# A transformer block on one NeuronCore: the attention's filling loaded and cast a tile in front, SyncE's queue in program order, and output pieces cast a product later

## The chip, the cores and the metric

One NeuronCore of a Trainium2 chip runs the whole program. The metric is the device time of one execution in microseconds; the median of several runs counts. The engines are TensorE (PE, matrix products), VectorE (DVE), ScalarE (ACT), GpSimd (POOL) and SyncE (SP, which here only issues transfers). Each works through its own instructions in their order, and they wait for one another by semaphores.

## The reference

One layer on x of 1 x 1024 x 1024 in float32:

```python
def reference(x, ...):
    h = rms_norm(x, ln1_g)
    proj = h @ w_in + b_in
    rq, rk, rv, rg, aq, ak, av, gate_a, gate_b = split(proj)  # 512 512 1024 1024 1024 128 128 1024 1024
    ry = head_group_norm(retention_chunkwise(rotary(rq), rotary(rk), rv), ret_norm_g)   # 4 heads
    branch_a = (silu(rg) * ry) @ w_ret_out
    ay = sliding_window_sink_attention(rotary(aq), rotary(ak), av, attn_sinks)  # 16 q, 2 kv heads, window 128
    branch_b = ay @ w_attn_out
    merged = sigmoid(gate_a) * branch_a + sigmoid(gate_b) * branch_b
    x = x + merged @ w_out
    h2 = rms_norm(x, ln2_g)
    x = x + (silu(h2 @ w_gate) * (h2 @ w_up)) @ w_down
    return rms_norm(x, lnf_g)
```

## The kernel before

Every float32 operand of a product is held as two numbers of a shorter format, a high part (a cast on ScalarE, the copy in `split`, line 133) and a low part (the difference, on VectorE, line 136). A product is the sum of three matmuls: high by high, high by low, low by high (lines 160 to 162 in `mm_g`). A weight slab of 1024 x 128 is loaded by SyncE into one of two raw buffers (`wr`), split into `wh` and `wl`, and used in 16 steps of three matmuls, eight steps for each half of the 1024 tokens.

The stage that the change concerns is the attention. The 16 query heads come in four quads. `quad_q(g)` makes the query projection of quad g: 32 steps on two slabs, with a rotation on VectorE (lines 440 to 449: six multiplies and adds and two low parts) for each half of the tokens. The results go out to `q_d` by four stores (line 452) and come back in another layout by four loads (line 453). `gate(n)` is one tile of the gates (16 steps), with a tanh whose result goes to `tb_d`.

Attention itself runs in 32 units (four quads by eight blocks of 128 queries). In turn i of the loop TensorE does `u_transpose` of unit i-2 (pT; ScalarE casts ph, VectorE makes pl at line 515 and the masked qh and ql at line 522), `u_scores` of unit i (s; exponentials at line 496), some steps of filling, and `u_values` of unit i-2 (pv, line 534, four matmuls that read ph, pl, qh and ql). From unit 16 on, `u_values` also adds halves and splits the sum on VectorE (lines 544 to 548). The filling is the projections of quads 1 to 3 and of twelve gate tiles, the gates 6 to 15, then 0 and 1: `Fill.step(n)` advances the generators by n steps, and `until(k)` runs them to the end of the k-th, so that a quad's queries are there when its first unit comes. TensorE's instructions are held in program order in this loop by `in_order`; SyncE's are placed by the scheduler. In turn 20 the four loads of `wv` (the retention's value weights) are issued, and in odd turns from 25 on VectorE subtracts quarters of it (line 593). What is left of the filling runs after the last unit (`fl.rest()`).

After the attention come the V products (va, vb; Strassen's scheme with seven products P1 to P7, whose sums of h VectorE makes into `vacc`, lines 660 and 663), then the W products of the retention's query, key and gate weights (wA, wB, wC; ten column blocks of seven products, 12 matmuls each, line 884). Their loop holds VectorE, ScalarE and GpSimd in program order. At the end of it, from product P6 of block 8 on, each product carries one piece of work for the attention's output: `split_ay(n)` reads a 128 x 512 piece of ay, adds its two parts on VectorE (`ays`, line 927), casts the sum on ScalarE (line 928), and one product later makes its low part on VectorE (line 922). Then follow `load_g(0)` and `k_transpose(0)` (kTT, transposes of the first retention head's keys) and the retention with the products of `w_attn_out` (acc_bb) as filling.

Of the kernel before, what the change touches and what calls it, by code (L numbers as in the profile page):

```python
# [17 lines left out]
P = 128  # L18
# [17 lines left out]
def f32(t):  # L36
    return t.bitcast(F32)
# [3 lines left out]
def hybrid_block(ctx: ExitStack, tc: tile.TileContext, x, ln1_g, w_in, b_in, ret_norm_g, w_ret_out,  # L41
# [262 lines left out]
    with tc.tile_pool(name="gt", bufs=1, side="right") as gt, tc.tile_pool(name="w1", bufs=1) as w1:  # L304
# [99 lines left out]
                ak_evac(q // 2, kb[q // 2])  # L404
                av_evac(q // 2, vb[q // 2])

        def quad_q(g):
            if g % 2 == 0:
                big(B, "B", g // 2, f"q{g}")
            Bt = B[g // 2]  # L410
            jb = (g % 2) * 4
            w = [hl_tiles([8, P], f"aq{g}{z}") for z in range(2)]
            hp = tc.high_priority(offset=AHEAD)
            hp.__enter__()
            for kk in range(2):
                raw = raw_slab([4, 256], f"aq{g}{kk}")
                nc.sync.dma_start(raw, w_in[kk * 512:kk * 512 + 512, C_AQ + g * 256:C_AQ + g * 256 + 256]
                                  .rearrange("(k p) n -> p k n", p=P))
                rv_ = raw.rearrange("p k (j z e) -> p k z j e", j=4, z=2, e=32)
                for z in range(2):  # L420
                    hi = w[z][0][:, kk * 4:kk * 4 + 4, :].rearrange("p k (j e) -> p k j e", e=32)
                    lo = w[z][1][:, kk * 4:kk * 4 + 4, :].rearrange("p k (j e) -> p k j e", e=32)
                    nc.scalar.copy(hi, rv_[:, :, z])
                    nc.vector.tensor_tensor(out=lo, in0=rv_[:, :, z], in1=f32(hi), op=ALU.subtract)
            hp.__exit__(None, None, None)
            ab = {}
            for half, z in ((0, 0), (0, 1), (1, 0), (1, 1)):
                pt = acc(f"aq{g}{z}{half}")
                yield from mm_g(pt, w[z], H, half * 512)
                t = r512("rab", 3, f"q{g}{z}{half}")  # L430
                nc.scalar.activation(t, pt, AF.Identity, bias=bcol[:, QB + 4 * z + g:QB + 4 * z + g + 1], scale=1.0)
                ab[z, half] = t
                if z == 0:
                    yield
                    continue
                c = slice(half * 512, half * 512 + 512)
                a, b = ab[0, half], t
                s1, s2 = (r512(f"st{i}", 1, f"st{i}{g}{half}") for i in (1, 2))
                cos, sin = atab[:, 0, c], atab[:, 1, c]
                nc.vector.tensor_tensor(out=s2, in0=a, in1=cos, op=ALU.mult)  # L440
                nc.vector.tensor_tensor(out=s1, in0=b, in1=sin, op=ALU.mult)
                nc.vector.tensor_tensor(out=s2, in0=s2, in1=s1, op=ALU.subtract)
                nc.vector.tensor_tensor(out=a, in0=a, in1=sin, op=ALU.mult)
                nc.vector.tensor_tensor(out=b, in0=b, in1=cos, op=ALU.mult)
                nc.vector.tensor_tensor(out=b, in0=b, in1=a, op=ALU.add)
                nc.scalar.activation(a.bitcast(F32R), s2, AF.Copy)
                nc.vector.tensor_tensor(out=s2.bitcast(F32R), in0=s2, in1=a, op=ALU.subtract)
                nc.scalar.activation(s1.bitcast(F32R), b, AF.Copy)
                nc.vector.tensor_tensor(out=b.bitcast(F32R), in0=b, in1=s1, op=ALU.subtract)
                qd = q_d[2 * g + half]  # L450
                for r, sr in ((0, a), (2, s2), (1, s1), (3, b)):
                    nc.sync.dma_start(qd[:, r, :], sr)
                    nc.sync.dma_start(f32(Bt[r * 32:r * 32 + 32, jb:jb + 4, c]),
                                      qd[:, r, :].rearrange("(j e) c -> e j c", e=32))
                yield
# [91 lines left out]
            nc.scalar.copy(v[:, :, 0, :], tm)  # L547
            nc.vector.tensor_tensor(out=v[:, :, 1, :], in0=tm, in1=f32(v[:, :, 0, :]), op=ALU.subtract)

        def gate(n):  # L550

            def evac(half, pt):
                t = gt.tile([P, 512], F32, tag="st", bufs=2, name=f"tb{n}{half}")
                nc.scalar.activation(t, pt, AF.Tanh, bias=bhalf[:, n:n + 1], scale=0.5)
                nc.sync.dma_start(tb_d[n, :, half * 512:half * 512 + 512], t)
            return dense_g(w_in, C_GA + n * P, H, evac, f"g{n}")

        run(quad_q(0))
        order = list(range(6, 16))
        gens = []  # L560
        for g in range(4):
            gens += [quad_q(g + 1)] if g < 3 else []
            gens += [gate(n) for n in (order[2 * g:2 * g + 2] if g < 3 else order[6:] + [0, 1])]
        fl = Fill(gens)
        NU = 4 * NB
        fl.step(20)
        left = 32 * 8 - 8 - 20
        with in_order(nc.tensor.engine):
            for i in range(NU + 2):
                if i % NB == 0 and 0 < i < NU:  # L570
                    fl.until(3 * (i // NB - 1) + 1)
                if i > 1:
                    u_transpose(i - 2)
                if i < NU:
# [341 lines left out]

    aysum = []

    def split_ay(n):
        if aysum:  # L920
            t, hi, lo = aysum.pop()
            nc.vector.tensor_tensor(out=lo, in0=t, in1=f32(hi), op=ALU.subtract)
        if n < 8:
            c = slice(n % 2 * 512, n % 2 * 512 + 512)
            hi, lo = AY[0][:, n // 2 * 2, c], AY[0][:, n // 2 * 2 + 1, c]
            t = ps("pv", 1, f"ays{n}")
            nc.vector.tensor_tensor(out=t, in0=f32(hi), in1=f32(lo), op=ALU.add)
            nc.scalar.copy(hi, t)
            aysum.append((t, hi, lo))

    qTs, kTs, kts, rgs = {}, {}, {}, {}
# [1 line left out]
    def load_kq(h, z):  # L933

        t = (kTs, qTs)[z][h] = kq.tile([P, S], F32, tag=("kT", "qT")[z], name=f"r{z}{h}")
        nc.sync.dma_start(t, rk_d[4 - 4 * z + h])

    with in_order(nc.vector.engine, nc.scalar.engine, nc.gpsimd.engine):
        for i, (j, pr) in enumerate(wseq):
            wprep_to(i + 3)  # L940
            wnow[0] = i
            wproduct(j, pr)
            while wlater and wlater[0][0] <= i:
                wlater.pop(0)[1]()
            if i >= wseq.index((8, "P6")):
                split_ay(i - wseq.index((8, "P6")))
            if (j, pr) == (7, "P6"):
                load_ay(0)
            elif (j, pr) == (8, "P5"):
                load_kq(0, 0)  # L950
                load_kq(0, 1)
            if (j, pr) == (NW - 2, "P5"):
                load_mask(0)
                load_v(0, 0)
                load_v(0, 1)
            if (j, pr) == (NW - 1, "P7"):
                load_ay(1)
        assert not wlater
# [173 lines left out]

    load_g(0)
    k_transpose(0)
    fl = Fill([bb_g(n) for n in range(8)])
    last = None
    for h in range(RH):
# [820 lines left out]
```

## Time and profile before

| what | us |
|---|---|
| median of 3 runs (1573.33 to 1576.23) | 1574.33 |
| the profiled execution | 1572.68 |
| its span | 1570.9 |
| TensorE busy in it (98%) | 1546.1 |
| VectorE busy (66%) | 1029.7 |
| ScalarE busy (45%) | 704.1 |
| GpSimd busy (25%) | 385.9 |
| first quad's projection starts | 42.35 |
| first attention unit's scores | 78.33 |
| last unit's values end, tail of the filling starts | 322.92 |
| V products start | 350.14 |

A row of a timeline has the start, the duration, the engine, the line of the kernel, the operation, what it writes and reads, and in brackets how long the engine was idle before it and what ended that. TensorE's matmuls overlap: one is recorded with 0.39 us, though the next one starts 0.227 us after it. A row of the waits has the waiting engine, tile and line, what it waited for, and the total, the count and the longest in us. A row of the windows has for each engine the busy time and the number of instructions, then the clock that was granted to TensorE (1.00 is full), the share of the transfer engines and GB/s.

### The profile page before, as it was taken

The page shows a single profiled execution, that of the slowest core. Times are in us where ns is not written, and L with a number is a line of the kernel's source. Part 1 is how long each engine was busy: PE and PEld are TensorE (multiplying, and loading weights), DVE is VectorE, ACT ScalarE, POOL GpSimd, SP SyncE. Part 2 cuts the span into 40 slices and gives each one's busy share as a digit, 9 for nine tenths or more (in the row PEclk, how much of TensorE's full clock was granted, in tenths as well). Part 3 has the DMA queues.
Part 4 walks back from the last instruction along what each step waited for, and adds up shares of the span by engine and source line. Part 5 has one row for each costly group of instructions (what it writes and reads, how often), then busy time and mean ns, then how long its engine had stood idle before and what let it go on. Part 6 is the DMA issues. An engine that isn't in the chain of part 4 may idle for free.

```text
span 1570.9 us, 20538 instructions
## 1 busy us (share of the span) xinstructions
PE 1546.1 (98%) x7323; PEld 1288.7 (82%) x7323; DVE 1029.7 (66%) x1670; ACT 704.1 (45%) x1436; POOL 385.9 (25%) x336
## 2 busy tenths in 40 slices
PE   9979999999999999999999999999999999999998
PEld 8868888888888886888888888888888888888886
DVE  6567888778557665787556789444444444678756
ACT  6346677733233344544223366333333333444445
POOL 2001110000054441000021123655555555100001
PEclk9999999999999999999999999999999999999999
DMA  6563655340475454664555402333333333863233
GB/s 219 178 201 121 192 183 163 113 141 29 146 199 165 141 164 150 230 206 161 173 185 179 187 1 81 119 109 101 101 101 109 113 101 101 286 256 86 96 103 125
DMA packets 156355, 228.34 MB, mean 145 GB/s; under 512 B 10011, under 2 KB 82525, under 8 KB 155998
## 3 DMA queue, kind: packets, MB, share of 16 engines
q1 hardware_dynamic: 154972, 222.85, 43.9%
q0 software_dynamic: 1280, 4.20, 0.8%
q8 instruction: 57, 0.93, 0.2%
q14 instruction: 44, 0.36, 0.1%
q10 hardware_dynamic: 2, 0.00, 0.0%
HBM read 152.29 MB, written 69.99 MB: 142 GB/s over the span
## 4 chain that ended last, share of the span: by engine, by line
PE 58%; DVE 1%; ACT 0%; DMA 0%; issue 0%; POOL 0%; POOLq 0%; ACTq 0%
PE fA L1582 15%; PE fB L1582 8%; PE dA L1884 7%; PE dxP L1884 6%; PE fC L1582 4%; PE wo L1416 3%; PE woP L1416 2%; PE acc_ba L162 2%; PE acc_ba L160 2%; PE acc_ba L161 2%; PE acc_bb L160 2%; PE acc_bb L161 2%; PE acc_bb L162 2%; PE rs L1020 0%; PE h2T L1346 0%; DMA r<-rk_d 0%
## 5 line engine op out<-in xcount | busy, mean ns | idle before, releaser
L1884 PE MATMUL dA<-dwP,daP 128*128 128x512 f32 x528 | 120.6, 389 | 0.0
L1884 PEld LDWEIGHTS dA<-dwP,daP 128*128 128x128 f32 x528 | 99.1, 188 | 20.7 <-DVE dwP L136 0.2
L1884 PE MATMUL dxP<-dwP,daP 128*128 128x512 f32 x396 | 90.2, 389 | 0.0
L1884 PEld LDWEIGHTS dxP<-dwP,daP 128*128 128x128 f32 x396 | 74.4, 188 | 15.4
L160 PE MATMUL acc_g<-h,wh_g 128*128 128x512 f32 x192 | 75.8, 395 | 8.1 <-ACT wh_g L133 8.1
L162 PE MATMUL acc_g<-h,wl_g 128*128 128x512 f32 x192 | 75.3, 392 | 0.4 <-DVE wl_g L136 0.4
L161 PE MATMUL acc_g<-h,wh_g 128*128 128x512 f32 x192 | 75.2, 392 | 0.0
L472 POOL COPY sc<-nsink 128x4 f32<-128x4 f32 x32 | 10.6, 332 | 243.7 <-PE pT L512 115.9
L1657 POOL TENSOR_TENSOR xf<-xf 128x512 f32<-128x512 f32 x40 | 61.1, 1527 | 30.4 <-issue 28.9
L496 ACT ACTIVATE sc<-sc,nm 128x129 f32<-128x129 f32 x128 | 50.1, 394 | 40.0 <-DVE nm L488 31.9
L1588 POOL TENSOR_TENSOR xf<-xf 128x512 f32<-128x512 f32 x33 | 47.3, 1435 | 58.5 <-ACT xf L1590 26.9
L136 DVE TENSOR_TENSOR dwP<-wd,dwP 128x512 fp32r<-128x512 f32 x77 | 52.9, 687 | 4.9 <-ACT dwP L133 4.9
L1789 POOL TENSOR_TENSOR rs_f<-tot,mhalf 128x1 f32<-128x1 f32 x8 | 4.8, 606 | 205.4 <-DVE tot L1786 205.4
L598 POOL TENSOR_TENSOR wr_wp<-wr_wp 128x512 f32<-128x512 f32 x10 | 15.7, 1572 | 146.9 <-DVE w0P L136 127.5
L133 ACT CAST dwP<-wd 128x512 fp32r<-128x512 f32 x77 | 47.4, 616 | 9.3 <-PE dA L1884 7.0
L160 PE MATMUL acc_bb<-ay,wh_bb 128*128 128x512 f32 x128 | 50.9, 399 | 0.0
L133 ACT CAST daP<-daP 128x512 fp32r<-128x512 f32 x42 | 26.0, 620 | 54.7 <-PE dxP L1884 26.7
L161 PE MATMUL acc_bb<-ay,wh_bb 128*128 128x512 f32 x128 | 50.2, 392 | 0.0
L162 PE MATMUL acc_bb<-ay,wl_bb 128*128 128x512 f32 x128 | 50.2, 392 | 0.0
L160 PE MATMUL aq<-h,wh_aq 128*128 128x512 f32 x128 | 50.1, 391 | 0.0
L161 PE MATMUL aq<-h,wh_aq 128*128 128x512 f32 x128 | 49.9, 390 | 0.0
L162 PE MATMUL aq<-h,wl_aq 128*128 128x512 f32 x128 | 49.9, 390 | 0.0
(845 smaller groups left out, 4361.5 us busy)
## 6 DMA issues: line engine op xcount, KB each, us to landing
act_d<-xf SPq DMA_DIRECT2D x77, 256.0 KB, 2.1
daP<-act_d SPq DMA_DIRECT2D x21, 512.0 KB, 3.7
q<-q_d SPq DMA_DIRECT2D x32, 256.0 KB, 4.6
wr_daP<-act_d SPq DMA_DIRECT2D x14, 512.0 KB, 3.7
wr_g<-in_w_in SPq DMA_DIRECT2D x12, 512.0 KB, 5.5
tb_d<-tb SPq DMA_DIRECT2D x24, 256.0 KB, 2.1
wd<-in_w_ffn_down SPq DMA_DIRECT2D x6, 1024.0 KB, 13.3
wr_f<-in_w_ffn_gate SPq DMA_DIRECT2D x11, 512.0 KB, 4.1
```

Of the source, the lines that this page charges most:

```text
L133: nc.scalar.copy(hi, raw)
L136: return nc.vector.tensor_tensor(out=lo, in0=raw, in1=f32(hi), op=ALU.subtract)
L160: nc.tensor.matmul(pt, hi[:, k, :], xh, start=(k == 0), stop=False)
L161: nc.tensor.matmul(pt, hi[:, k, :], xl, start=False, stop=False)
L162: nc.tensor.matmul(pt, lo[:, k, :], xh, start=False, stop=(k == 7))
L496: nc.scalar.activation(sc[:, j, 0:P + 1], sc[:, j, 0:P + 1], AF.Exp, scale=-1.0, bias=nm[:, j:j + 1], accum_out=den[:, j:j + 1])
L598: nc.gpsimd.tensor_tensor(out=o, in0=a, in1=b, op=ALU.subtract)
L1416: nc.tensor.matmul(bank, v[:, q + u, k, c], w[y][:, k % 2, :], start=(first and z == 0), stop=(last and z == 2), skip_group_check=not tracked)
L1582: nc.tensor.matmul(pt, o[:, w, k, :], v, start=(first and n == 0), stop=(n == 11), skip_group_check=not first)
L1588: nc.gpsimd.tensor_tensor(out=aq[q], in0=aq[q], in1=sg[q], op=ALU.mult)
L1657: nc.gpsimd.tensor_tensor(out=o, in0=a, in1=b, op=op)
L1884: nc.tensor.matmul(banks[tt], a[:, u, c], w[:, v, :], start=(fresh and f + z == 0), stop=(f == NP - 1 and z == 2), skip_group_check=not fresh)
```

## The change

In the attention's filling a quad and a gate become objects with `load()`, `prep()` and `products()`. `load_ahead()` loads raw slabs as far ahead as the two buffers allow (a quad takes both). `prep()` makes high and low parts: a gate's, or the first half of a quad's, during the item before (in its step 23 if that is a quad, in its first step if a gate); the second half of a quad's at its own start. The order of items becomes quad 1, gate 6, quad 2, gate 7, quad 3, gates 8 to 15, 0 and 1 (before: quad 1, gates 6 and 7, quad 2, gates 8 and 9, quad 3, gates 10 to 15, 0 and 1), with deadlines to match. The units take 244 steps in all instead of 228, 7.18 a unit instead of 6.7, so that 24 steps instead of 40 stand after the last unit. SyncE's instructions in this loop are held in program order. The stores of a query half are written ahead of its four reloads. `split_ay` makes the cast one product later than the sum, ahead of that product, and the low part behind it. TensorE is held in program order from the W products to the transposes of the first head's keys.

```diff
+        class QuadQ:
+            raws, size = 2, 2
...
+            def load(self):
+                for kk in range(2):
+                    raw = raw_slab([4, 256], f"aq{self.g}{kk}")
+                    nc.sync.dma_start(raw, w_in[...])
+                    self.raw.append(...)
+            def prep(self):
+                z = len(self.w)
+                self.w.append(hl_tiles([8, P], f"aq{self.g}{z}"))
+                for kk in range(2):
+                    ...
+                    nc.scalar.copy(hi, self.raw[kk][:, :, z])
+                    nc.vector.tensor_tensor(out=lo, in0=self.raw[kk][:, :, z], in1=f32(hi), op=ALU.subtract)
...
+        class Gate:
+            raws, size = 1, 1
...
+            def prep(self):
+                self.w.append(hl_tiles([8, P], f"g{self.n}"))
+                split(self.raw, *self.w[0])
...
                 for r, sr in ((0, a), (2, s2), (1, s1), (3, b)):
                     nc.sync.dma_start(qd[:, r, :], sr)
+                for r in (0, 2, 1, 3):
                     nc.sync.dma_start(f32(Bt[r * 32:r * 32 + 32, jb:jb + 4, c]),
...
-        run(quad_q(0))
-        order = list(range(6, 16))
-        gens = []
-        for g in range(4):
-            gens += [quad_q(g + 1)] if g < 3 else []
-            gens += [gate(n) for n in (order[2 * g:2 * g + 2] if g < 3 else order[6:] + [0, 1])]
-        fl = Fill(gens)
+        order = list(range(6, 16)) + [0, 1]
+        items = [QuadQ(0), QuadQ(1), Gate(order[0]), QuadQ(2), Gate(order[1]), QuadQ(3)] + [Gate(n) for n in order[2:]]
+        loaded = [0, 0]
+        def load_ahead():
+            while loaded[0] < len(items) and loaded[1] + items[loaded[0]].raws <= 2:
+                items[loaded[0]].load()
+                loaded[1] += items[loaded[0]].raws
+                loaded[0] += 1
+        def prep(it):
+            it.prep()
+            if len(it.w) == it.size:
+                loaded[1] -= it.raws
+            load_ahead()
+        def filling(n):
+            it = items[n]
+            late = it.size == 2
+            while len(it.w) < it.size:
+                prep(it)
+            for k, _ in enumerate(it.products()):
+                if k == (23 if late else 0) and n + 1 < len(items):
+                    prep(items[n + 1])
+                yield
+        load_ahead()
+        prep(items[0])
+        run(filling(0))
+        fl = Fill([filling(n) for n in range(1, len(items))])
         NU = 4 * NB
         fl.step(20)
-        left = 32 * 8 - 8 - 20
-        with in_order(nc.tensor.engine):
+        left = 32 * 8 - 8 - 4
+        with in_order(nc.tensor.engine, nc.sync.engine):
             for i in range(NU + 2):
                 if i % NB == 0 and 0 < i < NU:
-                    fl.until(3 * (i // NB - 1) + 1)
+                    fl.until((1, 3, 5)[i // NB - 1])
...
-    def split_ay(n):
-        if aysum:
+    def split_ay(n, front):
+        if front and aysum:
+            t, hi, lo = aysum[0]
+            nc.scalar.copy(hi, t)
+        elif not front and aysum:
             t, hi, lo = aysum.pop()
             nc.vector.tensor_tensor(out=lo, in0=t, in1=f32(hi), op=ALU.subtract)
-        if n < 8:
+        if not front and n < 8:
...
             nc.vector.tensor_tensor(out=t, in0=f32(hi), in1=f32(lo), op=ALU.add)
-            nc.scalar.copy(hi, t)
             aysum.append((t, hi, lo))
...
+    pinned = in_order(nc.tensor.engine)
+    pinned.__enter__()
     with in_order(nc.vector.engine, nc.scalar.engine, nc.gpsimd.engine):
         for i, (j, pr) in enumerate(wseq):
             wprep_to(i + 3)
             wnow[0] = i
+            piece = i - wseq.index((8, "P6"))
+            if piece >= 0:
+                split_ay(piece, True)
             wproduct(j, pr)
...
-            if i >= wseq.index((8, "P6")):
-                split_ay(i - wseq.index((8, "P6")))
+            if piece >= 0:
+                split_ay(piece, False)
...
     load_g(0)
     k_transpose(0)
+    pinned.__exit__(None, None, None)
```

In the rows of the programs' order the number behind a name is its buffer; `wr_g6` is the raw slab of gate 6, q100, st110, st210 and q110 are the rotated queries of quad 1's first half, q101 to q111 those of its second. SyncE's queue at the start of the attention, before:

```order
L453 DMA q0_650<-q_d_72 32x4x512 x4
L452 DMA q_d_72<-q100_856 128x512
L452 DMA q_d_72<-st210_886 128x512
L452 DMA q_d_72<-st110_885 128x512
L452 DMA q_d_72<-q110_883 128x512
L453 DMA q0_650<-q_d_72 32x4x512 x4
L149 DMA wr_g6_1031<-in_w_in 128x8x128
L452 DMA q_d_72<-q101_955 128x512
```

And with the change:

```order
L482 DMA q0_670<-q_d_72 32x4x512 x4
L440 DMA wr_g6_831<-in_w_in 128x8x128
L480 DMA q_d_72<-q100_858 128x512
L480 DMA q_d_72<-st210_888 128x512
L480 DMA q_d_72<-st110_887 128x512
L480 DMA q_d_72<-q110_885 128x512
L482 DMA q0_670<-q_d_72 32x4x512 x4
L416 DMA wr_aq20_963<-in_w_in 128x4x256
```

Gate 6's slab has moved from behind the first half's stores and reloads to ahead of them, and quad 2's first slab follows where it stood. ScalarE near the end of the W products (w9P6, w9P7, w9P5 and w9P4 are the weights of block 9's products; ays4 to ays7 are pieces of ay), before:

```order
L928 CAST ay0_5344<-ays5_5620 128x512
L133 CAST w9P7_5623<-wr_wp90_5395 128x512
L871 ACTIVATE r900_5639<-r900_5639,bhalf_89 128x512
L928 CAST ay0_5344<-ays6_5644 128x512
L133 CAST w9P5_5647<-wr_wp90_5395 128x512
L889 COPY u29_5662<-wA9_5554 128x512
L928 CAST ay0_5344<-ays7_5665 128x512
L133 CAST w9P4_5668<-wp91_5396 128x512
```

And with the change:

```order
L133 CAST w9P7_5622<-wr_wp90_5395 128x512
L975 CAST ay0_5344<-ays5_5620 128x512
L924 ACTIVATE r900_5639<-r900_5639,bhalf_89 128x512
L133 CAST w9P5_5646<-wr_wp90_5395 128x512
L975 CAST ay0_5344<-ays6_5644 128x512
L942 COPY u29_5662<-wA9_5554 128x512
L133 CAST w9P4_5667<-wp91_5396 128x512
L975 CAST ay0_5344<-ays7_5665 128x512
```

Each weight's cast has changed places with the cast of a piece of ay. TensorE there, before:

```order
L988 MATMUL kTT00_5750<-ident_83,r00_5516 128x128 x4
L988 MATMUL kTT01_5757<-ident_83,r00_5516 128x128 x4
L884 MATMUL wB9_5692<-h0_111,w9P5_5647 128x512 x2
L884 MATMUL wA9_5554<-s23_3673,w9P7_5623 128x512 x12
L884 MATMUL wB9_5692<-h0_111,w9P5_5647 128x512 x10
L884 MATMUL wA9_5554<-h1_112,w9P4_5668 128x512 x12
L884 MATMUL wB9_5692<-s4h_3674,w9P3_5689 128x512 x12
```

And with the change:

```order
L937 MATMUL wA9_5554<-s23_3673,w9P7_5622 128x512 x12
L937 MATMUL wB9_5692<-h0_111,w9P5_5646 128x512 x12
L937 MATMUL wA9_5554<-h1_112,w9P4_5667 128x512 x12
L937 MATMUL wB9_5692<-s4h_3674,w9P3_5689 128x512 x12
L1048 MATMUL kTT00_5750<-ident_83,r00_5515 128x128 x4
L1048 MATMUL kTT01_5757<-ident_83,r00_5515 128x128 x4
```

The transposes have moved behind the last product, and the products stand in program order.

More of the change, by code (lines that the diff above doesn't have):

```diff
@@ L405, in hybrid_block, with __init__, products, load @@
                 av_evac(q // 2, vb[q // 2])
-        def quad_q(g):
+        class QuadQ:
+            raws, size = 2, 2
+            def __init__(self, g):
+                self.g, self.raw, self.w = g, [], []
+            def load(self):
+                for kk in range(2):
+                    raw = raw_slab([4, 256], f"aq{self.g}{kk}")
+                    nc.sync.dma_start(raw, w_in[kk * 512:kk * 512 + 512, C_AQ + self.g * 256:C_AQ + self.g * 256 + 256]
+                                      .rearrange("(k p) n -> p k n", p=P))
+                    self.raw.append(raw.rearrange("p k (j z e) -> p k z j e", j=4, z=2, e=32))
+            def prep(self):
+                z = len(self.w)
+                self.w.append(hl_tiles([8, P], f"aq{self.g}{z}"))
+                for kk in range(2):
+                    hi, lo = (t[:, kk * 4:kk * 4 + 4, :].rearrange("p k (j e) -> p k j e", e=32) for t in self.w[z])
+                    nc.scalar.copy(hi, self.raw[kk][:, :, z])
+                    nc.vector.tensor_tensor(out=lo, in0=self.raw[kk][:, :, z], in1=f32(hi), op=ALU.subtract)
+            def products(self):
+                return quad_q(self.g, self.w)
+        class Gate:
+            raws, size = 1, 1
+            def __init__(self, n):
+                self.n, self.w = n, []
+            def load(self):
+                self.raw = raw_slab([8, P], f"g{self.n}")
+                c = C_GA + self.n * P
+                nc.sync.dma_start(self.raw, w_in[:, c:c + P].rearrange("(k p) n -> p k n", p=P))
+            def prep(self):
+                self.w.append(hl_tiles([8, P], f"g{self.n}"))
+                split(self.raw, *self.w[0])
+            def products(self):
+                return gate(self.n, self.w[0])
+        def quad_q(g, w):
             if g % 2 == 0:
@@ L411, in quad_q @@
             jb = (g % 2) * 4
[L412 to L425, printed above, removed]
             ab = {}
@@ L548, in u_values, with gate @@
             nc.vector.tensor_tensor(out=v[:, :, 1, :], in0=tm, in1=f32(v[:, :, 0, :]), op=ALU.subtract)
-        def gate(n):
-            def evac(half, pt):
+        def gate(n, w):
+            for half in range(2):
+                pt = acc(f"acc_g{n}_{half}")
+                yield from mm_g(pt, w, H, half * 512)
                 t = gt.tile([P, 512], F32, tag="st", bufs=2, name=f"tb{n}{half}")
@@ L555, in evac @@
                 nc.sync.dma_start(tb_d[n, :, half * 512:half * 512 + 512], t)
-            return dense_g(w_in, C_GA + n * P, H, evac, f"g{n}")
-        run(quad_q(0))
-        order = list(range(6, 16))
-        gens = []
-        for g in range(4):
-            gens += [quad_q(g + 1)] if g < 3 else []
-            gens += [gate(n) for n in (order[2 * g:2 * g + 2] if g < 3 else order[6:] + [0, 1])]
-        fl = Fill(gens)
+                yield
[20 more added lines that the diff above has]
+                    prep(items[n + 1])
+                yield
+        load_ahead()
+        prep(items[0])
+        run(filling(0))
+        fl = Fill([filling(n) for n in range(1, len(items))])
         NU = 4 * NB
         fl.step(20)
-        left = 32 * 8 - 8 - 20
-        with in_order(nc.tensor.engine):
+        left = 32 * 8 - 8 - 4
+        with in_order(nc.tensor.engine, nc.sync.engine):
             for i in range(NU + 2):
                 if i % NB == 0 and 0 < i < NU:
-                    fl.until(3 * (i // NB - 1) + 1)
+                    fl.until((1, 3, 5)[i // NB - 1])
                 if i > 1:
```

## The prediction

> **What bounds the kernel now.** I read the head of the page, then TensorE's waits, then the timelines of the engines at each of these waits.
>
> ```profile
> span 1570.9 us, 20538 instructions
> ...
> PE 1546.1 (98%) x7323; PEld 1288.7 (82%) x7323; DVE 1029.7 (66%) x1670; ACT 704.1 (45%) x1436; POOL 385.9 (25%) x336
> ...
> PE acc_g L160 <- ACT wh_g L133: 8.1, 1, 8.1
> PE wB L884 <- ACT w9P L133: 1.8, 1, 1.8
> PE kTT L988 <- DVE r L864: 1.4, 1, 1.4
> PE pv L534 <- DVE pl L515: 1.2, 1, 1.2
> ...
> PE pv L534 <- DVE qh L522: 1.0, 1, 1.0
> PE wA L884 <- ACT w9P L133: 0.6, 1, 0.6
> ...
> PE acc_g L162 <- DVE wl_g L136: 0.4, 1, 0.4
> ```
>
> TensorE is busy for 98% of the span, and all its idle time is 1570.9 - 1546.1 = 24.8 us. No matmul is added or removed, so the change can only move idle time and matmuls slowed by the clock. Seven waits, 14.5 us, lie where it works: at gate 6 (acc_g), in the values of two attention units (pv), and in the last W products (wA, wB, kTT). The profiled execution took 1572.68 us, span and 1.78 around it; the median of the runs, 1574.33, is 1.65 above that. I sum against the execution and carry the difference over to the median.
>
> The pace: in the tail of the attention TensorE runs 120 filling matmuls with no gap (the first row below is the first of them, the second row the V product after them; the DVE rows are used further down).
>
> ```profile
> 322.92 0.40 PE L160 MATMUL acc_g<-h,wh_g 128*128 128x512 f32 x1
> ...
> 350.14 2.22 PE L729 MATMUL va<-vP,h 128*128 128x512 f32 x9
> ...
> 325.74 2.36 DVE L660 TENSOR_TENSOR vacc<-h 128x1024 f32<-128x1024 f32 x2
> ...
> 330.42 1.22 DVE L136 TENSOR_TENSOR wl_g<-wr_g,wh_g 128x1024 fp32r<-128x1024 f32 x1
> 331.55 2.48 DVE L663 TENSOR_TENSOR vacc<-vacc 128x1024 f32<-128x1024 f32 x2
> ...
> 342.39 1.29 DVE L136 TENSOR_TENSOR vP<-wv,vP 128x512 fp32r<-128x512 f32 x2
> ```
>
> 27.22 / 120 = 0.227 us per 128x512 matmul; more between two starts than this is lost.
>
> **Gate 6: load and casts a tile in front, the queue as written.** Rows of the timelines of SyncE's queue, ScalarE, TensorE and VectorE, then a row of the windows (the third figure from its end is the clock granted) and the landing time of the slab.
>
> ```profile
> 77.04 3.77 SPq L453 DMA_DIRECT2D q<-q_d  x4
> ...
> 89.67 0.43 SPq L149 DMA_DIRECT2D wr_g<-in_w_in  x1
> ...
> 88.37 0.39 ACT L496 ACTIVATE sc<-sc,nm 128x129 f32<-128x129 f32 x1
> ...
> 88.23 0.39 PE L162 MATMUL aq<-h,wl_aq 128*128 128x512 f32 x1
> ...
> 96.67 0.80 PE L160 MATMUL acc_g<-h,wh_g 128*128 128x512 f32 x1 [8.06 <-ACT wh_g L133]
> ...
> 95.57 1.04 ACT L133 CAST wh_g<-wr_g 128x1024 fp32r<-128x1024 f32 x1 [0.62 <-DMA wr_g<-in_w_in]
> ...
> 96.65 1.23 DVE L136 TENSOR_TENSOR wl_g<-wr_g,wh_g 128x1024 fp32r<-128x1024 f32 x1 [0.89 <-ACT wh_g L133]
> ...
> 97.00:100.00 3.00, 2.96 (x10) 2.06 (x10) 0.88 (x1) 0.38 (x1) 0.19 (x1) 0.50 0.99 287
> ...
> DMA to landing us min/median/max: 5.9/5.9/5.9
> ```
>
> Gate 6's raw slab is issued at 89.67, when TensorE already stands still, since its issue comes behind the four q100 stores (they wait for VectorE's rotation) and those stores' reloads. It lands 5.9 later, is cast for 1.04, and TensorE starts at 96.67: 96.67 - 88.23 - 0.23 = 8.2 us lost. Then a clock window runs at half (0.50 in the row): 3.4 us of half speed, 1.7 us more. Together 9.9. Now the load stands ahead of those stores, right behind the reloads that end at 77.04 + 3.77 = 80.8, so it lands near 86.7. The hi cast stands on ScalarE behind the last exponential of unit 1 (88.37, with its accumulator read to about 88.8, some 0.3 later after the new neighbours), so it ends near 90.1 and the lo split near 91.3. TensorE gets there at 88.46 as before (the same 20 steps, 7 and 5), runs nothing of the gate until 90.1, and its third matmul starts at 91.35 where 88.92 would be free: 2.4 us remain. Gain 9.9 - 2.4 = 7.5. Ends: 5.8, if the 512 KB share the queues with quad 2's reloads and land 1.7 later; 9.9, if the cast slips in ahead of the exponentials; I take the chain of rows. Behind the waiting cast stand only the evacuations of quad 1 and unit 2's copies, and TensorE is ahead of neither. Gate 7's wait of 0.4 (with its edges 0.5) goes too: its split now runs during quad 2. The stores behind the moved loads lose nothing: their reloads serve unit 8 and later. Writing all four stores ahead of the four reloads costs nothing: the queue already ran them so (the reloads x4 are one group in the row at 77.04).
>
> **Quads closer.** Quads 2 and 3 come after gates 6 and 7, and so end by about unit 16; the deadline is until(5) for unit 24.
>
> ```profile
> 222.04 0.39 PE L534 MATMUL pv<-pl,vev 128*128 128x512 f32 x1
> ...
> 223.44 0.50 PE L534 MATMUL pv<-qh,vdf 128*128 128x512 f32 x1 [1.01 <-DVE qh L522]
> ...
> 237.12 0.39 PE L534 MATMUL pv<-ph,vev 128*128 128x512 f32 x1
> ...
> 238.73 0.49 PE L534 MATMUL pv<-pl,vev 128*128 128x512 f32 x1 [1.21 <-DVE pl L515]
> ...
> 220.56 0.69 DVE L515 TENSOR_TENSOR pl<-pT,ph 128x512 fp32r<-128x512 f32 x1
> ...
> 228.34 0.69 DVE L515 TENSOR_TENSOR pl<-pT,ph 128x512 fp32r<-128x512 f32 x1
> ...
> 237.98 0.69 DVE L515 TENSOR_TENSOR pl<-pT,ph 128x512 fp32r<-128x512 f32 x1
> ...
> 209.73 0.69 DVE L593 TENSOR_TENSOR wv<-wv 128x512 f32<-128x512 f32 x1 [2.01 <-DMA wv<-in_w_in]
> ...
> 262.36 0.60 PE L512 MATMUL pT<-ident,sc 128*128 128x128 f32 x4
> ...
> 269.45 0.60 PE L512 MATMUL pT<-ident,sc 128*128 128x128 f32 x4
> ...
> 236.60:240.00 3.40, 1.98 (x8) 0.86 (x6) 3.37 (x7) 0.50 (x2) 0.00 (x0) 1.00 0.85 296
> 240.00:243.40 3.40, 3.40 (x14) 3.20 (x15) 3.05 (x8) 2.55 (x10) 0.19 (x1) 0.50 0.96 243
> ```
>
> A unit with seven steps of filling takes TensorE 269.45 - 262.36 = 7.1 us. Between successive pl splits VectorE needed 7.8 (220.56 to 228.34) and 9.6 us (to 237.98): rotations of quad 3, gate splits, the wv subtractions, which had first waited 2.0, and the output sums that only units 16 and later have meet there. The price: 223.44 - 222.04 - 0.23 = 1.2 and its follower 0.4; 238.73 - 237.12 - 0.23 = 1.4 and three followers 1.0; the half clock from 240.0 to 243.4, 1.7 less what overlaps, 1.4: 5.4 in all. With the rows' pitches (0.60 for 128x512, 1.14 for a gate split) I added up VectorE's new order from pl to pl: the fullest units are 5 (7.5 us) and 12 (8.0, a rotation and gate 8's split), with neighbours of 3.8 to 6.3, and no rotation falls behind unit 16. From pl to the values that need it TensorE has some 3 us of other work, so one unit 0.9 over the pace is absorbed; the least margin by hand is 0.7 us, at unit 12's values. Taken: 5.2 of 5.4. Ends: 2, if unit 12 stalls as at 237; 5.6. The longer slices (7.18 steps a unit for 6.7) cost nothing by themselves; their matmuls leave the tail.
>
> **V products begin under a shorter tail.** After the last unit 24 steps remain where there were 40: 72 matmuls, 16.3 us. VectorE's twelve sums, which start 325.74 - 322.92 = 2.8 behind the last values, and the first vP low part follow in the old order; only the split wl_g between them (331.55 - 330.42 = 1.13) is earlier now. The first low part ends at 342.39 + 0.69 - 1.13 - 322.92 = 19.0. TensorE, with the four high-part matmuls that the new order puts first, needs it at 16.3 + 0.9 = 17.2. A new wait of 1.75; ends 0 (all sums at 1.14) and 2.5.
>
> **Output pieces cast a product later, TensorE pinned.**
>
> ```profile
> 601.15 3.29 PE L884 MATMUL wC<-h,w9P 128*128 128x512 f32 x12
> ...
> 617.24 1.07 PE L884 MATMUL wB<-h,w9P 128*128 128x512 f32 x4
> ...
> 608.78 0.69 DVE L136 TENSOR_TENSOR w9P<-wr_wp,w9P 128x512 fp32r<-128x512 f32 x1 [1.17 <-ACT w9P L133]
> ...
> 610.71 0.70 DVE L927 TENSOR_TENSOR ays<-ay 128x512 f32<-128x512 f32 x1
> ```
>
> Per product it is a ring: the sum ays on VectorE, its cast on ScalarE, the weight's cast behind that, the weight's low part on VectorE (which stood idle 1.17 for the cast), then r, the piece's low part, and the next ays at 610.71. From 608.78 to 610.71 + 0.70 is 2.6 us of work without a pause, and with the 1.17 the ring is 3.8 us against 12 x 0.227 = 2.7 of matmuls. From 601.15 to 617.24 are 38 matmuls (8.6) and eight transposes (0.7) in 16.1 us: 6.8 lost, a half-clock window among it. Now the weight's cast stands first and the 1.17 goes; VectorE's 2.6 fits under 2.7 by 0.1, and pieces without an r by 0.7. The transposes kTT stand behind the last product. Gain 6.6, ends 4.5 (VectorE slowed by GpSimd in one piece and one clock window left) and 7.3 (with the losses just ahead). What is late next is the second half of ay, which is loaded when the ring ends: it moves with it. Retention's first head gets another interleaving of the same matmuls; the nearest waits there are 0.5 and less: zero, ends -1 and +1.
>
> **The clock at the new waits.** A half-clock window is 1.7. One followed a window in which TensorE was busy 1.98 of 3.40 (236.60 above); 1.55 lost at 222 was followed by none. Waits of 2.4 (gate 6) and 1.75 (V) lie about there: I take one of the two, 1.7.
>
> The Trainium skill, page "TensorE: Matmul & The Clock Gate", section "What's actually happening", has the clock halve after an idle window of about 3.4 us. The trace differs: the window at 236.60 was 58% busy. By that rule neither wait would halve it, and the sum would be 1.7 us lower.
>
> **Sum.** -7.5 - 0.5 - 5.2 + 1.75 - 6.6 + 1.7 = -16.35. Execution 1572.68 - 16.35 = 1556.3, median 1558.0.
>
> **Rivals.**
> - No halved clock at either new wait, the rest as summed: 1558.0 - 1.7 = 1556.3. For it: 222; against: 236.6. This is also what the skill's rule gives.
> - VectorE falls short in units 5 to 15 of about half of the units, since all three quads now lie there: half of the slower case's 24 us below, 12, less than the gain, 1570; two or three stalled units, 1563 to 1566. For it: 220 to 238; against: the counts above.
> - The W tail stays bound by VectorE (2.6 against 2.7 leaves nothing for a slow row): gain 3 instead of 6.6, 1561.6.
> - Slower: VectorE's backlog carries over from unit to unit, because each unit's rotation stands in front of its own pl. All twelve units of quads 1 to 3 then lose what 222 and 237 lost, (1.55 + 2.4) / 2 = 2.0 each: 24 us, 16.35 - 24 = 7.6 slower, 1582. It decides when VectorE's rows pass 7.1 us in most units; my counts say in two.
> - It does not do what it says: with SyncE's queue in program order a load stands behind a store that isn't ready, as wr_g did, at another gate; 8 us at one place, 1566, and at two about no change.
>
> **How the numbers follow.** Measurement tells about 0.2%, 3.1 us, from no change. The forecast of 1553 to 1563 has 0.60 (0.2 of it the first rival), the W tail 0.08, two or three stalled units or one blocked load (1563 to 1566) 0.13, both ends good (1551 to 1553) 0.05, 1566 to 1571 0.04, no change 0.04, slower 0.06. From 1551 to 1566 is 0.86. Faster 0.90, same 0.04, slower 0.06.
>
> **What the new profile would show.** wr_g issued near 81 and gate 6 waiting 2 to 3 us for wh_g and wl_g; no pv wait over 0.3; va waiting for vP's low part 1 to 2.5; no wB or wA wait at the last products. A pv wait in units 5 to 14, an acc_g wait for a load or a halved clock in more than one new place would make it wrong.

## The result, and the profile after

The changed kernel took 1556.78 us in the median (1555.69 to 1557.95) against 1574.74 of the kernel before (four runs of each): a ratio of 0.9886, with an interval of 0.9869 to 0.9903. It is faster by about 18 us, where 16.35 had been summed and 1558.0 forecast. In a second series it took 1558.17 (ratio 0.9903, 0.9886 to 0.9920). The profiled execution took 1556.4 us. The head of the page of the changed kernel:

```profile
span 1554.5 us, 20543 instructions
...
PE 1540.6 (99%) x7323; PEld 1287.0 (83%) x7323; DVE 1020.8 (66%) x1670; ACT 704.6 (45%) x1436; POOL 389.7 (25%) x336
```

Its TensorE waits (what waited, for what, the total, the count and the longest in us):

```profile
PE acc_g L160 <- ACT wh_g L133: 1.7, 1, 1.7
PE va L782 <- DVE vP L136: 1.1, 1, 1.1
PE warm L269 <- DVE wk L243: 1.0, 1, 1.0
PE wA L937 <- ACT u L942: 0.7, 1, 0.7
PE acc_g L162 <- DVE wl_g L136: 0.5, 1, 0.5
...
PE va L782 <- ACT tb L584: 0.4, 1, 0.4
```

TensorE's idle time fell from 24.8 to 1554.5 - 1540.6 = 13.9 us. The 8.1 at gate 6 has become 1.7 and 0.5, the pv, wB and kTT waits are gone, and two new ones stand at the start of the V products (va).

Where the time went is read from the first matmul of each stage. All later tables give the same differences to the profile before, each stage from the first matmul of the one ahead (start: up to the first quad; attention: to the first V product; V: to the first W product; W: to the first scores of the retention; rest: to the last matmul). The median of the runs stands beside them.

| kernel | start | attention | V | W | rest | span | median |
|---|---|---|---|---|---|---|---|
| changed | +2.28 | -14.05 | +2.04 | -6.90 | +0.18 | 1554.5 | 1556.78 |
| changed, again | +0.63 | -14.04 | +3.67 | -6.99 | +0.07 | 1554.3 | 1558.17 |

The start is not touched by the change, but the first quad begins anywhere from 42.15 to 44.63 us in the thirteen profiles. Five of them record a half-clock window there, which opens at 7.1 to 8.5 us; in the four that begin latest, the changed kernel's among them, the record of the clock opens only at about 13 us. Behind the start the changed kernel is 18.7 us ahead.

Gate 6 in the changed kernel: SyncE's queue, TensorE, ScalarE, VectorE (the timelines).

```profile
78.29 2.96 SPq L482 DMA_DIRECT2D q<-q_d  x4
81.30 0.43 SPq L440 DMA_DIRECT2D wr_g<-in_w_in  x1
...
90.46 0.39 PE L162 MATMUL aq<-h,wl_aq 128*128 128x512 f32 x1
92.54 0.50 PE L160 MATMUL acc_g<-h,wh_g 128*128 128x512 f32 x1 [1.69 <-ACT wh_g L133]
...
93.80 0.50 PE L162 MATMUL acc_g<-h,wl_g 128*128 128x512 f32 x1 [0.53 <-DVE wl_g L136]
...
91.37 0.19 ACT L525 ACTIVATION_READ_ACCUMULATOR sc<-sc,nm 128x1 f32 x1
91.46 1.03 ACT L133 CAST wh_g<-wr_g 128x1024 fp32r<-128x1024 f32 x1
...
92.52 1.23 DVE L136 TENSOR_TENSOR wl_g<-wr_g,wh_g 128x1024 fp32r<-128x1024 f32 x1
```

The slab is issued at 81.30 right behind the reloads, 8.4 us earlier than before (10.65 counted from the first quad), and now the cast waits for no transfer: it stands behind the last exponential of unit 1 (91.37). The V products and the W tail, TensorE and then VectorE:

```profile
338.37 0.84 PE L782 MATMUL va<-vP,h 128*128 128x512 f32 x3
339.60 0.50 PE L782 MATMUL va<-vP,h 128*128 128x512 f32 x1 [0.39 <-ACT tb L584]
341.23 0.95 PE L782 MATMUL va<-vP,h 128*128 128x512 f32 x3 [1.12 <-DVE vP L136]
...
597.90 3.02 PE L937 MATMUL wA<-s,w9P 128*128 128x512 f32 x12 [0.68 <-ACT u L942]
600.75 2.88 PE L937 MATMUL wB<-h,w9P 128*128 128x512 f32 x12
...
340.49 1.29 DVE L136 TENSOR_TENSOR vP<-wv,vP 128x512 fp32r<-128x512 f32 x2
...
593.86 0.69 DVE L136 TENSOR_TENSOR w9P<-wr_wp,w9P 128x512 fp32r<-128x512 f32 x1
594.54 0.69 DVE L917 TENSOR_TENSOR r<-wC,p 128x512 f32<-128x512 f32 x1
595.15 0.68 DVE L978 TENSOR_TENSOR ay<-ays,ay 128x512 fp32r<-128x512 f32 x1
595.87 0.70 DVE L983 TENSOR_TENSOR ays<-ay 128x512 f32<-128x512 f32 x1
596.58 0.69 DVE L136 TENSOR_TENSOR w9P<-wr_wp,w9P 128x512 fp32r<-128x512 f32 x1
```

VectorE's four steps of a piece follow one another without the idle 1.17: from one w9P to the next, 593.86 to 596.58, is 2.72 us, the time of twelve matmuls.

### The profile page after: what moved, and what is told of

Read it like the earlier page. It is cut to its first block, busy times and chain, and to the rows that moved or that the text cites. A ratio compares the mean times of both kernels' runs of the same rounds, so it can differ in the third digit from the quotient of the medians.

```text
span 1554.5 us, 20543 instructions
## 1 busy us (share of the span) xinstructions
PE 1540.6 (99%) x7323; PEld 1287.0 (83%) x7323; DVE 1020.8 (66%) x1670; ACT 704.6 (45%) x1436; POOL 389.7 (25%) x336
## 4 chain that ended last, share of the span: by engine, by line
PE 95%; DVE 3%; ACT 1%; issue 1%; POOL 0%; POOLq 0%; DVEq 0%; ACTq 0%
PE fA L1643 15%; PE fB L1643 8%; PE dA L1945 7%; PE wA L937 7%; PE dxP L1945 6%; PE fC L1643 4%; PE wB L937 3%; PE wo L1477 3%; PE va L782 3%; PE acc_g L162 2%; PE acc_g L160 2%; PE acc_g L161 2%; PE woP L1477 2%; PE vP L782 2%; PE aq L160 2%; PE aq L161 2%
```

## The experiments

**The W tail alone.** The kernel before, with the later cast and the pinned TensorE, the attention as it was:

```diff
...
-            nc.scalar.copy(hi, t)
...
+    pinned = in_order(nc.tensor.engine)
+    pinned.__enter__()
...
+            if piece >= 0:
+                split_ay(piece, True)
             wproduct(j, pr)
...
+            if piece >= 0:
+                split_ay(piece, False)
...
+    pinned.__exit__(None, None, None)
```

> The kernel before with only the W tail's part of the change: the cast of a piece of ay a product later, TensorE pinned there; the attention as before. Theory (four separate terms): 5.5 to 6.6 us faster than before (about 1568.5), the acc_g wait of 8.1 us and the two pv waits as before, one wait of 0.7 left at the last W products. Rival (the parts lean on each other, the tail gains only because the attention hands over earlier): less than 3 us.

Median 1566.12, ratio 0.9951 (0.9935 to 0.9967); W -5.82, rest +0.20, and the wait of 0.7 for u as forecast. The tail's part needs nothing of the attention's. The median gained 8.0 where 5.5 to 6.6 were expected, and of the two pv waits that should have stayed only the second did, the first shrank to 0.1; the attention's -1.60, in code that was not changed, is taken up below the table of stages.

**Its two halves.** The later cast without the pin (the edit against the run above), and the pin without the later cast (against the kernel before):

```diff
-    pinned = in_order(nc.tensor.engine)
-    pinned.__enter__()
...
-    pinned.__exit__(None, None, None)
```

> The kernel before with only the later cast in split_ay, TensorE's order left to the scheduler. Theory (the ring of sum, cast, weight's cast and low part is what was lost): as tail_only within 1 us, 5.5 to 6.6 us faster, no VectorE idle of 1.17 per product. Rival (the order of TensorE, with the transposes kTT ahead of the last products, is what was lost): 2 us or less.

```diff
+    pinned = in_order(nc.tensor.engine)
+    pinned.__enter__()
...
+    pinned.__exit__(None, None, None)
```

> The kernel before with only TensorE pinned from the W products to the transposes, the cast of a piece still right behind its sum. Theory: the ring stays at 3.8 us a product, so at most 2 us faster, with a wait for w9P of about 1 us in each of the last products. Rival (TensorE's order): 5 us or more faster.

The later cast alone: 1567.99, ratio 0.9957 (0.9945 to 0.9969), W -6.47. That is 1.9 behind tail_only where 1 had been expected, all of it in the start and the attention, which neither edit touches. The pin alone: 1574.91, ratio 1.0004 (0.9993 to 1.0015), W +1.66. The theory of the ring holds. VectorE and TensorE with the pin alone (timelines):

```profile
609.97 0.69 DVE L136 TENSOR_TENSOR w9P<-wr_wp,w9P 128x512 fp32r<-128x512 f32 x1 [1.17 <-ACT w9P L133]
...
614.28 5.49 PE L884 MATMUL wA<-s,w9P 128*128 128x512 f32 x12 [4.79 <-ACT u L889]
```

VectorE with the later cast alone, and a row of its waits:

```profile
604.29 0.69 DVE L136 TENSOR_TENSOR w9P<-wr_wp,w9P 128x512 fp32r<-128x512 f32 x1
```

```profile
PE acc_bb L160 <- DMA ay<-ay_d: 0.9, 1, 0.9
```

With the pin alone the ring keeps its 1.17, and the transposes, which had filled 0.7 us of the gap, can no longer do so: TensorE waits 4.79 in one piece, put down to u but behind the ring's casts on ScalarE, and 5.9 us at half clock follow (614.28 to 620.15). With the later cast alone the scheduler lays four matmuls of P5 between P6 and P7. That spares the 0.7 for u, since P7 adds to the bank that the copy u reads; but P7 ends later, and the load of the second half of ay, which starts behind it, is 0.9 late. With the pin it is the other way round. The pin by itself is worth nothing that these runs tell.

**Quads apart.** The changed kernel, with the items in the old order:

```diff
-        items = [QuadQ(0), QuadQ(1), Gate(order[0]), QuadQ(2), Gate(order[1]), QuadQ(3)] + ...
+        items = [QuadQ(0)]
+        for q in range(1, 4):
+            items += [QuadQ(q)] + [Gate(n) for n in order[2 * q - 2:2 * q]]
+        items += [Gate(n) for n in order[6:]]
...
-                    fl.until((1, 3, 5)[i // NB - 1])
+                    fl.until((1, 4, 7)[i // NB - 1])
```

> The changed kernel with the items in the order of the kernel before (quad 1, gates 6 and 7, quad 2, gates 8 and 9, quad 3, the other gates), all else as changed. Theory (quad 3's rotations meet the output sums of units 16 and later on VectorE): 2 to 5.5 us slower than the changed kernel (1559 to 1562), with pv waits of about 1 us for pl or qh in units 16 to 20. Rival (the waits at 222 and 237 came from the late wv load and the scheduler's queue): within 1 us of the changed kernel, no pv wait.

Median 1559.09, ratio 0.9904 (0.9886 to 0.9922), attention -10.20. It is slower than the changed kernel, as the theory wanted, but for other reasons: no pv wait is among its waits. Its 3.85 us are a half-clock window at gate 6 (1.7, last section), 0.45 and 0.76 at the start of quad 2, whose casts come late in that order, and small waits. So the rotations of quad 3 among the output sums of units 16 and later did not by themselves make the waits at 222 and 237, and the mechanism that I had written down was not complete. What differs from the kernel before on VectorE, as far as the timelines show, is where the wv subtractions stand and that quad 3's second rotation ends at 229.6 in place of 237.6:

```profile
L649 DVE TENSOR_TENSOR wv<-wv x4: 679/682/685, 260.9 to 267.6; 128x512 f32<-128x512 f32 x4
```

That is the row of the tile wv in this run: the subtractions come at 260.9 to 267.6, since SyncE in program order issues the loads behind the queries, at 234.8 in place of 190.0; before the change they began at 209.73, after 2.01 of waiting.

**Quads apart and SyncE free; SyncE free alone.** So both, and the other single one:

```diff
-        with in_order(nc.tensor.engine, nc.sync.engine):
+        with in_order(nc.tensor.engine):
```

> The changed kernel with the items in the old order and SyncE's instructions in the attention placed by the scheduler again; casts a tile in front and 7.18 steps a unit stay. The scheduler then issues the four wv loads ahead of quad 3's last stores, and VectorE's wv subtractions stand in units 17 to 21 among quad 3's rotations, as before the change (with SyncE in program order they stand in units 26 and later, or behind unit 20). Theory (either of the two cures the waits at units 17 and 19, since both the rotations and the wv subtractions are needed for them): one or two pv waits of 0.5 to 1.3 us come back, 1 to 4 us slower than quads_apart. Rival 1 (7.18 steps a unit alone gives VectorE the time): no pv wait over 0.3, as quads_apart within 1 us. Rival 2 (SyncE's order sets gate 6): a wait of 8 us at acc_g.

> The changed kernel with SyncE's instructions in the attention placed by the scheduler; everything else as changed. Gate 6's slab stands at the same place in its queue as in the changed kernel, the wv loads stand earlier and between other transfers. Theory (gate 6's gain comes from loading ahead, and the quads' new places alone already keep units 17 and 19 free): within 1 us of the changed kernel, attention from the first quad to the last values within 0.7 us. Rival (the queue's order carries the gain): 5 us or more slower.

Quads apart with SyncE free: 1561.53, ratio 0.9915 (0.9895 to 0.9934), attention -8.92. The wait is back, from VectorE's and TensorE's timelines:

```profile
208.25 0.69 DVE L649 TENSOR_TENSOR wv<-wv 128x512 f32<-128x512 f32 x1 [1.96 <-DMA wv<-in_w_in]
...
230.19 0.69 DVE L551 SCALAR_TENSOR_TENSOR qh<-amask,ph 128x512 fp32r<-128x512 f32 x1
...
230.93 0.49 PE L563 MATMUL pv<-qh,vdf 128*128 128x512 f32 x1 [1.64 <-DVE qh L551]
```

VectorE waits 1.96 for wv in the middle of the rotation, and two units later TensorE loses 1.9 and 0.4. Less its half-clock window quads_apart had lost 2.15 to the changed kernel, this run 5.13; the difference, 3.0, is what the free queue costs in the old order. In the new order it costs little: SyncE free alone gives 1558.12, ratio 0.9893 (0.9873 to 0.9913), attention -13.28, 0.8 from the changed kernel and no pv wait over 0.11. By the medians it is 1.3, where within 1 had been expected. So either edit, the new places of the quads or SyncE in program order, keeps units 17 and 19 free. The subtractions themselves stood late in each of the runs without the wait, though, in the last one too:

```profile
L646 DVE TENSOR_TENSOR wv<-wv x4: 659/683/684, 236.1 to 239.5; 128x512 f32<-128x512 f32 x4
```

That is the row of the tile wv with SyncE free alone. No run has the quads early and the subtractions at 209 as well, so whether early quads would bear them there is not shown. What the longer slices do here isn't shown either: both runs with the quads late have 7.18 steps a unit. Gate 6 starts at 47.91 us from the first quad in all three as in the changed kernel: the hold on SyncE's order has no part in that.

**No casts in front.** The changed kernel, each item casting at its own start:

```diff
-                if k == (23 if late else 0) and n + 1 < len(items):
-                    prep(items[n + 1])
```

> The changed kernel without the casts in front: each item makes its own high and low parts at its start, and so the next load also comes an item later where a quad is the next; gate 6's slab keeps its place. Theory (gate 6 gains from its early load; the casts in front are needed at the starts of quads 2 and 3): gate 6 waits the same 2 us, quad 2 and quad 3 each start 1 to 4 us late, 2 to 6 us slower than the changed kernel. Rival (loads ahead suffice): within 1 us.

Median 1573.12, ratio 0.9991 (0.9980 to 1.0001): all but nothing of the gain is left, and 16.3 us are lost to the changed kernel where I had expected 2 to 6. Attention +3.78, 17.8 more than in the changed kernel. TensorE, SyncE's queue and ScalarE at the start of quad 2, and then a window in that wait:

```profile
107.72 0.28 PE L510 MATMUL s<-kst,q 128*128 128x256 f32 x1
112.90 0.79 PE L160 MATMUL aq<-h,wh_aq 128*128 128x512 f32 x1 [4.90 <-ACT wh_aq L425]
...
98.53 2.70 SPq L482 DMA_DIRECT2D q<-q_d  x4
101.28 0.98 SPq L416 DMA_DIRECT2D wr_aq<-in_w_in  x2
...
112.25 1.64 ACT L425 CAST wh_aq<-wr_aq 128x512 fp32r<-128x512 f32 x3
```

```profile
110.80:114.20 3.40, 1.30 (x3) 0.77 (x4) 1.98 (x5) 3.40 (x12) 0.00 (x0) 0.50 0.01 4
```

Quad 2's slabs are issued at 101.28, behind the q101 stores and reloads, in place of 91.95, and cast behind the exponentials of a unit: 5.1 lost. Quad 3 loses 4.3 in the same way, a gate 2.0, and in each of the two quads' waits a half clock begins that lasts two windows. TensorE works in it from 112.90 to 117.65 and from 166.22 to 172.27, 10.8 us at half speed, which cost 5.4: 5.1 + 4.3 + 2.0 + 5.4 = 16.8 of the 17.8. Gate 6 waits the same 1.7 as in the changed kernel. So its own gain comes from the early load. The new order of the quads needs the work in front, but since `prep()` also starts the next loads, this run takes away the early casts and the quads' early loads together, and does not tell them apart.

**A tail of 40 steps.** The changed kernel with the old spacing:

```diff
-        left = 32 * 8 - 8 - 4
+        left = 32 * 8 - 8 - 20
```

> The changed kernel with 40 steps of filling left behind the last unit, as before the change, and 6.7 a unit. Theory (the 24 steps are too short a cover for VectorE's sums): the wait for vP's low part and the one behind tanh at the start of the V products, 1.95 us together, go, and no unit stalls: 1.5 to 2 us faster than the changed kernel. Rival (longer slices are what keeps VectorE in time in units 5 and 12): pv waits of 1 us in these units, and no gain.

Median 1556.19, ratio 0.9882 (0.9860 to 0.9904): V +0.01, so both waits at the V products are gone, 2.03 us. But attention is -12.70, 1.35 less gained, lost mainly behind qh and ql in units 25 and 30, up to 0.4 at a time. In the profile 0.7 remains of it, and in the medians nothing that can be told.

**Gate 6 cast first, and both.** Two manual orders place unit 1's exponentials (e, ScalarE) behind gate 6's high part and its reciprocal (r, VectorE) behind the low part. The last two lines are in both only: 28 steps behind the last unit.

```diff
...
+                    if u == 1:
+                        behind(e, first_gate[6][0])
...
+            if u == 1:
+                behind(r, first_gate[6][1])
...
-        left = 32 * 8 - 8 - 4
+        left = 32 * 8 - 8 - 8
```

> The changed kernel once more, as the measure for the two beside it: 1557 us within 1; the halved clock and the clock at the start may fall differently, gate 6 waits 1.7 + 0.5 and the V products 0.4 + 1.1 again.

> The changed kernel with gate 6's high part made ahead of unit 1's exponentials on ScalarE, and its low part ahead of unit 1's reciprocal on VectorE. Theory (the slab lies ready from about 87, and the casts only stand behind work that itself waits for VectorE): acc_g waits 0.5 or less in all instead of 2.5 lost, 1.8 to 2.4 us faster than the changed kernel. Rival (the exponentials pushed back stall the unit's transposes): the loss moves to pT, within 0.5 us of the changed kernel.

> gate6_first with 28 steps of filling behind the last unit instead of 24. Theory: the V products' waits go as well (1.95 lost), no pv wait over 0.3 appears: 3.5 to 4.5 us faster than the changed kernel, near 1553. Rival (as in tail40, what is gained at the V products is given back in the units): 2 to 2.5 us faster, as gate6_first.

In one series with the changed kernel (1558.17, where 1557 within 1 had been expected): gate6_first 1554.06, ratio 0.9877 (0.9863 to 0.9892); both 1553.30, 0.9877 (0.9861 to 0.9894). Gate 6 in gate6_first, ScalarE and TensorE:

```profile
88.06 1.06 ACT L452 CAST wh_g<-wr_g 128x1024 fp32r<-128x1024 f32 x1
89.90 0.41 ACT L534 ACTIVATE sc<-sc,nm 128x129 f32<-128x129 f32 x1 [0.78 <-DVE nm L526]
...
90.69 0.39 PE L160 MATMUL acc_g<-h,wh_g 128*128 128x512 f32 x1
...
91.38 0.50 PE L162 MATMUL acc_g<-h,wl_g 128*128 128x512 f32 x1
```

The cast fits into ScalarE's pause, the exponentials start at 89.90 as in the changed kernel, and TensorE loses 0.24 in place of 2.54; attention -16.20, 2.15 better than the changed kernel. both takes the V waits away as well (V +0.01), but attention is -13.96: the 2.1 gained at V are given back in the units, as the rival said. A row of its TensorE in unit 25:

```profile
273.36 0.49 PE L576 MATMUL pv<-qh,vdf 128*128 128x512 f32 x1 [0.25 <-DVE qh L564]
```

All of them by stage:

| kernel | start | attention | V | W | rest | span | median |
|---|---|---|---|---|---|---|---|
| tail_only | +0.63 | -1.60 | 0.00 | -5.82 | +0.20 | 1564.3 | 1566.12 |
| late_no_pin | +2.25 | -0.60 | 0.00 | -6.47 | +0.11 | 1566.2 | 1567.99 |
| pin_no_late | +0.62 | +0.15 | +0.03 | +1.66 | +0.14 | 1573.5 | 1574.91 |
| quads_apart | +0.38 | -10.20 | +2.06 | -5.85 | +0.14 | 1557.4 | 1559.09 |
| apart_free | -0.20 | -8.92 | +2.06 | -5.90 | +0.20 | 1558.2 | 1561.53 |
| sync_free | +2.26 | -13.28 | +2.08 | -5.97 | +0.16 | 1556.2 | 1558.12 |
| no_prep_ahead | +0.16 | +3.78 | +2.07 | -4.15 | +0.28 | 1573.0 | 1573.12 |
| tail40 | +0.50 | -12.70 | +0.01 | -7.51 | +0.10 | 1551.3 | 1556.19 |
| gate6_first | +2.28 | -16.20 | +2.10 | -6.26 | +0.26 | 1553.1 | 1554.06 |
| both | -0.08 | -13.96 | +0.01 | -6.99 | +0.49 | 1550.4 | 1553.30 |

Attention varies by 1.75 where it wasn't touched (tail_only, late_no_pin, pin_no_late), and that variation is an experiment by itself. VectorE's wait for wv is not the same in each execution, as in tail_only:

```profile
209.36 0.69 DVE L593 TENSOR_TENSOR wv<-wv 128x512 f32<-128x512 f32 x1 [0.90 <-DMA wv<-in_w_in]
```

With waits of 0.90 (tail_only), 1.22 (late_no_pin), 2.01 (pin_no_late) and 2.01 (the kernel before) unit 17 loses 0.4, 0.8, 1.55 and 1.55. So the loss at unit 17 goes with the wait for wv, in the same code. Unit 19 loses 2.1 in all four, and a half clock follows it in two of them. What holds unit 19 is therefore not the length of that wait; whether it is the subtractions standing among the rotations or the rotations alone, no run tells.

W varies too among the runs that have the same edit there, from -5.82 to -7.51 (no_prep_ahead has -4.15): waits of TensorE for low parts of block 2's weights (w2P), 0.1 to 0.4 each and 0.7 at most, come and go. The best of these kernels, gate6_first and both, stand 4.1 and 4.9 us below the changed one in the same series, though their intervals just touch its own; between the two no difference can be told.

## Why the prediction was right, point by point

- **Gate 6**, -7.5. Right in place, size and rest: landing 5.6 behind the issue, then the cast behind unit 1's exponentials, a rest of 1.85 + 0.69 = 2.54 lost (2.4). Gate 7's 0.5 went. That the issue came at 81.30 (near 81 forecast) is in part chance: this execution began 2.28 later, so counted from the first quad the issue was 1.8 earlier than forecast. The exponentials set the cast, so it changed nothing.
- **Quads closer**, -5.2. The attention gained 14.05; less 9.9 - 2.5 at gate 6 and 0.5 at gate 7 that leaves 6.2 for units 17 and 19 and small waits. Size nearly right, 1.0 above the term; the cause was at most half of it. I had listed the wv subtractions and their wait of 2.0 among VectorE's load and then given the gain to the quads' places. The new places weren't needed: with SyncE in program order the waits are gone with the quads late as well (quads_apart). Unit 17's loss follows the wait for wv; what exactly held unit 19 stays open. That the size came out is in part luck, since the change makes both edits.
- **Casts a tile in front**: the step that I did not price. The sum counts 0.5 for gate 7; without the casts, and with the quads' loads an item later, 17.8 us of attention are lost. I put that down to the new order, which brings quads 2 and 3 to TensorE only 16 steps behind the quad before; no run has the new code in the old order without the casts. It did no harm to the forecast, since the change has both.
- **V products**, +1.75: 2.04 measured. 1.40 is the wait for the low part; the other 0.55, a matmul that waits for the last gate's tanh (tb), I hadn't seen. The low part alone would have come out 0.35 under the term.
- **W tail**, -6.6: -6.9 in the changed kernel, -5.8 by itself, with 1.7 of variation between runs. The ring was the cause, as pin_no_late and late_no_pin show. That no wA wait would be left was wrong: 0.84 stays between P6 and P7 of the last block, which the pin puts side by side on one bank.
- **The clock**, +1.7 for one of two new waits: none in the profile of the changed kernel, one (at V) in its second, which is the 3.67 in its row.
- **Retention**, 0: +0.2.
- The rivals: VectorE's backlog in the closer quads did not come, no pv wait over 0.1 in units 5 to 16. SyncE's order blocked no load. That both halvings would be spared, as the prediction worked out by the rule it cites from the Trainium skill, came true in one profile and not in the other.

Summed from the first quad on the forecast is -16.35, and -18.7 and -17.3 are measured; the 2.35 between it and the first are the clock (1.7), 0.85 more in the attention and 0.3 in the tail, less 0.3 at V and 0.2 in the rest. That the profiled execution, 1556.4, meets the sum's 1556.3 is luck: its later start of 2.28 makes up for the 2.35.

## What to carry to other kernels

A wait can go by either of two edits, so a wait that stays away when one edit is undone does not show that the edit was idle: undo them one by one and together, and look at what else each of them moved (here the subtractions, in every run without the wait). A stretch that no edit touched, and that still differs between executions, shows causes too. Look at who stands in front of a cast, not only at when its data land: a cast that was ready 4 us early still stood behind four exponentials that themselves were waiting. Filling that is taken from one place to cover a wait is missing at the other: here four more steps in the tail gained 2.1 at V and lost 2.2 in the units (both against gate6_first), and sixteen gained 2.0 and lost 1.35 (tail40).

## What the runs showed of the hardware that I had not expected

The clock's windows are 3.41 us long, and whether the next one runs at half is told neither by idle time nor by TensorE's busy share. Rows of the windows from four profiles, each window and the one behind it: the kernel before (near 237), pin_no_late and quads_apart (both near gate 6), the changed kernel again (V).

```profile
236.58:239.99 3.41, 1.99 (x8) 0.87 (x6) 3.38 (x7) 0.52 (x2) 0.00 (x0) 1.00 0.85 294
239.99:243.41 3.42, 3.42 (x14) 3.21 (x15) 3.07 (x8) 2.56 (x10) 0.19 (x1) 0.50 0.97 246
```

```profile
87.67:91.08 3.41, 1.57 (x7) 0.95 (x6) 2.36 (x7) 2.27 (x9) 0.00 (x0) 1.00 0.95 282
91.08:94.49 3.41, 0.00 (x0) 0.00 (x0) 3.24 (x5) 0.06 (x1) 0.00 (x0) 1.00 0.96 260
```

```profile
89.06:92.47 3.41, 1.29 (x4) 0.78 (x5) 2.71 (x4) 3.06 (x7) 0.00 (x0) 1.00 0.87 217
92.47:95.88 3.41, 3.41 (x15) 3.10 (x14) 3.41 (x6) 0.96 (x2) 0.24 (x1) 0.50 0.40 94
```

```profile
336.75:340.16 3.41, 1.90 (x7) 1.03 (x6) 3.38 (x5) 2.62 (x4) 0.00 (x0) 1.00 0.21 77
340.16:343.57 3.41, 3.41 (x9) 2.67 (x8) 3.34 (x3) 0.60 (x2) 0.00 (x0) 0.50 0.00 0
```

The second pair was busy for 1.57 us and kept the full clock in the next window; the first was busy for 1.99 and the fourth for 1.90, and both were followed by 0.50. A lone matmul is recorded longer (0.50 and more) than the 0.227 that it takes in a row, so I counted the columns of the matmuls that started in each window instead, in units of 512. In the thirteen profiles, between the start and the last products, windows at full clock with up to 5 units were followed by half clock each time (eleven windows, 0 to 5), and windows with 6 and more were not, but for one with 6 (236.58), whose sixth started 0.06 us before the window's end. That is a count over these runs, not a tested rule. The Trainium skill, page "TensorE: Matmul & The Clock Gate", section "What's actually happening", names an idle window as the condition; the trace agrees for the windows with no matmul, and shows halving behind windows with up to five as well. What it means for a kernel: the same wait of 2.5 us at gate 6 was followed by a half clock in one of six profiles, depending on where the windows fell.
